# Where split weights begin inside their SBUF tiles: three lines or one, by unit and by part

## The chip, the core and the metric

The kernel runs on one core of a Trainium2 chip. The metric is the device time of one launch in microseconds (us); lower is better. Three runs of the kernel before gave 573.05, 573.16 and 573.88 us, median 573.16.

## What is computed

A decoder trunk of two layers on 256 tokens of width 1024, in float32. Layer 0 mixes tokens by a gated short convolution, layer 1 by causal attention with rotary positions (all 256 tokens lie in one block, so the block selection of the reference selects nothing more). Each layer ends in a gated MLP with a width-3 causal convolution. Cut to what matters:

```python
for i in range(DEPTH):                      # DEPTH = 2, D = 1024, D_FF = 2816
    h = rmsnorm(x, mix_norm[i])
    x = x + (short_conv_mixer(h, ...) if i == 0 else moba_attention(h, w_qkv, w_o))
    gu = causal_dwconv(rmsnorm(x, ffn_norm[i]) @ ffn_w_up[i], ffn_w_conv[i])
    g, u = split(gu, 2)
    x = x + (silu(g) * u) @ ffn_w_down[i]
return rmsnorm(x, final_norm)
```

## The kernel before

**Weights.** All weights lie in one array, cut into 201 units of 128 partitions by up to 1024 columns (`PLAN`), in the order in which they are used: the first and further units of the layer-0 mixer (`first`, `in`, `out`), the MLP of layer 0 (`up`, `down`), then `q`, `k` and `v` in four groups of four heads, then eight units `o`, then the MLP of layer 1. A chunk of two units is fetched by one DMA from the SP queue into a tile `raw`, four chunks ahead. `split_next` makes two float32r tiles of a unit: `hi` by a copy on ScalarE (ACT), `lo` = raw - hi by a subtraction on VectorE (DVE). Five tiles of each kind turn round (`SPLITS`).

**Products.** Every product is made of three matmuls, hi x hi, hi x lo and lo x hi (`passes`). The activations are split in the same way (`xh`/`xl`, `ps` and `o` with h and l). Where the weight is *held*, TensorE loads a 128 x 128 piece of the weight (LDWEIGHTS, the row PEld of the profile) and lets 256 columns of the activation run through it. In the stages `v` and `down` of layer 1 it is the other way: the weight is *streamed*, 512 columns at a time, and a 128 x 128 piece of the activation is loaded. These are `v_stage` and `TokenAccum.add`. A load runs beside the matmul before it.

**Places.** A tile of split weights is 1152 float32 columns long and begins at a multiple of 512 bytes. Inside it the 1024 columns of the weight begin some columns later: `HELD_AT` puts held weights at column 48 (hi) and 16 (lo), which is three and one lines of 64 bytes beyond the multiple of 512, and `STREAMED_AT` puts streamed ones at column 64, four lines, in both parts. A piece of 128 columns is 512 bytes long, so each piece of a unit stands at the same distance beyond a multiple of 512. All activations begin at such a multiple (`INPUTS_AT` is 0 throughout).

**Order.** Each engine executes its instructions in the order in which the code writes them (`InOrder` ties each instruction to the one before on its engine). In the attention, other kinds of matmul stand between the units of q, k, v and o: scores `s`, transposes `pt` and values `o` (not to be confused with the weights `o`, whose results are named `ao`). The MLP of layer 1 begins with ten units `up` (results `gu`) before its first unit `down` (results `fo`); from then on two units `up` and one unit `down` take turns.

The profile names nearly all instructions by one line, since a helper records them: tile names tell them apart. `qk`, `v`, `ao`, `gu`, `fo`, `cv`, `b` and `mo` are accumulators in PSUM.

Of the kernel before, what the change touches and what calls it, by code (L numbers as in the profile page):

```python
# [33 lines left out]
LINE = 128  # L34

HELD_AT = {"hi": 48, "lo": 16}
STREAMED_AT = {"hi": 64, "lo": 64}  # L40
INPUTS_AT = {0: 0, "out": 0, 1: 0, "down0": 0, 2: 0, "o": 0, 3: 0, "down1": 0}
NPS = 7
WARM = 8
# [9 lines left out]
def weight_plan():  # L53

    plan = [("first", n) for n in range(len(FIRST))]
    for j in range(ND):
        if j > 1:
            plan += [("in", 0, 1, j), ("in", 0, 2, j), ("in", 0, 0, j)]
        if j >= LAG_MIX:
            plan.append(("out", 0, j - LAG_MIX))  # L60
    plan += [("out", 0, j) for j in range(ND - LAG_MIX, ND)]
    for layer in range(2):
        if layer == 1:
            for g in range(GROUPS):
                plan += [(n, g, half) for n in "qk" for half in range(2)]
                if g in (0, GROUPS - 1):
                    plan += [("v", g // 2, c) for c in range(4)]
            plan += [("o", m) for m in range(ND)]
        for j in range(NF):
            plan += [("up", layer, 0, j), ("up", layer, 1, j)]  # L70
            if j >= LAG_FFN:
                plan.append(("down", layer, j - LAG_FFN))
        plan += [("down", layer, j) for j in range(NF - LAG_FFN, NF)]
    return plan


PLAN = weight_plan()
INDEX = {k: i for i, k in enumerate(PLAN)}
NU = len(PLAN)
WIDTH = [P * len(FIRST[k[1]][1]) if k[0] == "first" else U for k in PLAN]  # L80
CHUNKS = [[0, 1, 2, 3, 4], [5, 6], [7, 8], [9, 10]]
while CHUNKS[-1][-1] + 1 < NU:
    _s = CHUNKS[-1][-1] + 1
    CHUNKS.append(list(range(_s, min(_s + 2, NU))))
CHUNK_OF = {u: (c, sum(WIDTH[v] for v in us if v < u)) for c, us in enumerate(CHUNKS) for u in us}
CHUNK_WIDTH = [sum(WIDTH[u] for u in us) for us in CHUNKS]
CHUNK_START = [P * sum(CHUNK_WIDTH[:c]) for c in range(len(CHUNKS))]
# [29 lines left out]
def trunk(ctx: ExitStack, tc: tile.TileContext, x, wall, small, ropes, masks, final, out):  # L117
# [21 lines left out]
    def line(pool, w, off=0, dtype=F32, **kw):  # L139

        return pool.tile([P, -(-(off + w) // LINE) * LINE], dtype, **kw)[:, off : off + w]
# [14 lines left out]
    raw, hi, lo = {}, {}, {}  # L156

    def load_chunk():
        c = state["dma"]
        state["dma"] += 1  # L160
        w = CHUNK_WIDTH[c]
        raw[c] = wp.tile([P, w], F32, name=f"raw{c}", tag="raw", bufs=LOADS)
        s = CHUNK_START[c]
        src = wall[s : s + P * w].rearrange("(p f) -> p f", p=P)
        cuts = [CHUNK_OF[u][1] for u in CHUNKS[c]] + [w] if c < 4 else [0, w]
        for a, b in zip(cuts, cuts[1:]):
            Q.dma_start(raw[c][:, a:b], src[:, a:b])
# [10 lines left out]
    def split_next():  # L178
        u = state["split"]
        if u >= NU:  # L180
            return
        state["split"] += 1
        c, o = CHUNK_OF[u]
        while state["dma"] <= min(c + LOADS - 1, len(CHUNKS) - 1):
            load_chunk()
        w = WIDTH[u]
        src = raw[c][:, o : o + w]
        at = STREAMED_AT if PLAN[u][0] == "v" or PLAN[u][:2] == ("down", 1) else HELD_AT
        hi[u], lo[u] = (
            line(wp, U + 127 - at[n], at[n], F32R, name=f"{n}{u}", tag=n, bufs=SPLITS)[:, :w]  # L190
            for n in ("hi", "lo")
        )
        if u < 2:
            V.tensor_copy(hi[u], src)
            if u == 0:
                scaled(0, (0,), nm0)
                split_next()
                for v, part in ((0, src), (1, raw[0][:, P : 3 * P])):
                    V.tensor_sub(lo[v], part, hi[v].bitcast(F32))
            return  # L200
        S.activation(hi[u], src, AF.Copy)
        V.tensor_sub(lo[u], src, hi[u].bitcast(F32))

    def unit(key):
        u = INDEX[key]
        while state["split"] <= u:
            split_next()
        return hi[u], lo[u]
# [7 lines left out]
    def slot(splits=1):  # L216
        for _ in range(splits):
            split_next()
        for g in sorted(tasks, key=lambda g: g.__name__ == "rotate"):
            if next(g, StopIteration) is StopIteration:  # L220
                tasks.remove(g)
# [36 lines left out]
    def scaled(i, ms, nm):  # L258

        for m in ms:  # L260
            xh, xl = (
                line(ap_, T, INPUTS_AT[i], F32R, name=f"x{c}{i}_{m}", tag=f"x{c}{m}", bufs=1)
                for c in "hl"
            )
            S.activation(xh, xslice(m), AF.Copy, scale=gain(i, m))
            V.scalar_tensor_tensor(
                xl, xslice(m), gain(i, m), xh.bitcast(F32), op0=ALU.mult, op1=ALU.subtract
            )
            nm.xh[m], nm.xl[m] = xh, xl

    def prep(i, pair, nm, splits=2):
        scaled(i, (2 * pair, 2 * pair + 1), nm)
        if pair:
            square(i, pair - 1, nm)
        if pair == 3:
            square(i, pair, nm)
            sums = sum_squares(i, nm)
            next(sums)
            for _ in range(splits):
                split_next()  # L280
            next(sums, None)
# [628 lines left out]
```

## Time and profile before

| what | value |
|---|---|
| median of three runs | 573.16 us |
| the profiled execution, device time | 573.11 us |
| its span, first to last instruction | 571.3 us |
| TensorE (PE) busy | 564.7 us, 99% of the span |
| weight loads (PEld) busy | 544.5 us, 95% |
| VectorE busy | 469.5 us, 82% |
| ScalarE busy | 337.4 us, 59% |
| mean share of the DMA engines | 52.4% for the queue of the weights |
| granted clock of TensorE over the span | 0.999 |

Matmuls overlap one another: the duration of one is longer than the distance to the next. So a busy share of 99% does not tell how fast the matmuls follow each other; that is read from the starts of two matmuls in the timeline, divided by the number of matmuls from the one to the other.

### The profile page before, as it was taken

To read this page: it belongs to the slowest core of one execution; us is meant where nothing else is said; L and a number is where in the kernel's file an instruction comes from. 1 tells how busy PE (TensorE), PEld (TensorE's weight loads), DVE (VectorE), ACT (ScalarE), POOL (GpSimd) and SP (SyncE) were. 2 spreads that over 40 slices of the span, in tenths; PEclk is the share of its full clock that TensorE was granted. 3 is DMA by queue.
4 is the path that set the end of the run, shared out by engine and by line. 5 is a ranking of instruction groups with operands and counts; after the bars stand their busy time and mean duration, and the time that the engine had idled before them with its cause. 6 is when DMAs were issued, how large, how long until landed. Compare 5 with 4: busy or idle time off the path is not lost.

```text
span 571.3 us, 11291 instructions
## 1 busy us (share of the span) xinstructions
PE 564.7 (99%) x4628; PEld 544.5 (95%) x4628; DVE 469.5 (82%) x783; ACT 337.4 (59%) x556; POOL 8.8 (2%) x12
## 2 busy tenths in 40 slices
PE   9999999999999999999999999999999999999996
PEld 9999999999999999999989997999999999999994
DVE  5998767999988888886998887577999778878883
ACT  6655447567755555555937666565665555555553
POOL 0022010000000000000000000000000000000000
PEclk9999999999999999999999999999999999999999
DMA  8966552746755556556364334463466465555301
GB/s 296 384 216 238 205 205 89 263 154 231 263 177 211 204 170 217 178 192 220 91 247 169 97 139 148 148 231 112 177 220 231 176 220 163 206 204 172 142 1 73
DMA packets 17188, 106.86 MB, mean 187 GB/s; under 512 B 1904, under 2 KB 3056, under 8 KB 4976
## 3 DMA queue, kind: packets, MB, share of 16 engines
q1 hardware_dynamic: 16704, 105.60, 52.4%
q8 instruction: 36, 0.59, 0.4%
q10 hardware_dynamic: 432, 0.54, 0.3%
q14 instruction: 16, 0.13, 0.1%
HBM read 105.09 MB, written 1.05 MB: 186 GB/s over the span
## 4 chain that ended last, share of the span: by engine, by line
PE 99%; ACT 0%; DVE 0%; issue 0%
PE gu L100 42%; PE fo L100 21%; PE qk L100 8%; PE cv L100 8%; PE ao L100 4%; PE b L100 4%; PE v L100 4%; PE mo L100 4%; PE pt L100 1%; PE s L100 1%; PE o L100 1%; PE busy L100 1%; PE ss L100 0%; ACT of L100 0%; DVE of L100 0%; ACT sq L100 0%
## 5 line engine op out<-in xcount | busy, mean ns | idle before, releaser
L100 ACT ACTIVATE hi<-raw 128x1024 fp32r<-128x1024 f32 (+2 forms) x199 | 205.1, 1041 | 146.2 <-PE gu L100 78.9
L100 DVE TENSOR_TENSOR lo<-raw,hi 128x1024 fp32r<-128x1024 f32 (+3 forms) x201 | 239.7, 1200 | 54.9 <-ACT hi L100 54.7
L100 PE MATMUL gu<-xl,hi 128*128 128x256 f32 x704 | 194.9, 277 | 0.0
L100 PE MATMUL gu<-xh,hi 128*128 128x256 f32 x704 | 194.6, 276 | 0.0
L100 PE MATMUL gu<-xh,lo 128*128 128x256 f32 x704 | 194.6, 276 | 0.0
L100 PEld LDWEIGHTS gu<-xh,hi 128*128 128x128 f32 x704 | 132.2, 188 | 0.7
L100 PEld LDWEIGHTS gu<-xl,hi 128*128 128x128 f32 x704 | 132.1, 188 | 0.6
L100 PEld LDWEIGHTS gu<-xh,lo 128*128 128x128 f32 x704 | 132.1, 188 | 0.0
L100 DVE SCALAR_TENSOR_TENSOR gy<-gn,sm,gy 128x255 f32<-128x255 f32 (+1 forms) x176 | 80.8, 481 | 3.1
L100 ACT ACTIVATE gy<-gn,sm 128x256 f32<-128x256 f32 x88 | 39.3, 497 | 6.6 <-DVE gn L100 6.5
L100 PE MATMUL qk<-xh,hi 128*128 128x256 f32 x128 | 36.0, 281 | 0.0
L100 PE MATMUL qk<-xl,hi 128*128 128x256 f32 x128 | 35.6, 278 | 0.0
L100 PE MATMUL qk<-xh,lo 128*128 128x256 f32 x128 | 35.4, 277 | 0.0
L100 DVE TENSOR_TENSOR gn<-gu,rstd 128x512 f32<-128x512 f32 x44 | 30.1, 688 | 5.1 <-PE gu L100 5.1
L100 PE MATMUL cv<-xh,hi 128*128 128x256 f32 x128 | 33.4, 282 | 0.0
L100 PE MATMUL cv<-xl,hi 128*128 128x256 f32 x128 | 32.9, 278 | 0.0
L100 PE MATMUL cv<-xh,lo 128*128 128x256 f32 x128 | 32.9, 278 | 0.0
L100 PEld LDWEIGHTS qk<-xh,hi 128*128 128x128 f32 x128 | 24.0, 188 | 0.5 <-issue 0.3
L100 PEld LDWEIGHTS qk<-xl,hi 128*128 128x128 f32 x128 | 24.0, 188 | 0.0
L100 PEld LDWEIGHTS qk<-xh,lo 128*128 128x128 f32 x128 | 24.0, 188 | 0.0
L100 ACT ACTIVATE s<-gy 128x256 f32<-128x256 f32 x44 | 17.9, 406 | 9.8 <-DVE gy L100 9.7
L100 PEld LDWEIGHTS cv<-xh,hi 128*128 128x128 f32 x128 | 23.4, 192 | 0.1
(474 smaller groups left out, 1075.1 us busy)
## 6 DMA issues: line engine op xcount, KB each, us to landing
raw<-wall SPq DMA_DIRECT2D x95, 1024.0 KB, 4.7
raw<-wall SPq DMA_DIRECT2D x6, 384.0 KB, 6.5
xt<-x SPq DMA_DIRECT2D x3, 256.0 KB, 6.0
out<-of SPq DMA_DIRECT2D x3, 256.0 KB, 2.1
raw<-wall SPq DMA_DIRECT2D x3, 192.0 KB, 4.1
gain_row<-final SPq DMA_DIRECT2D x1, 512.0 KB, 5.7
rope<-ropes SPq DMA_DIRECT2D x1, 384.0 KB, 5.3
out<-of ACTq DMA_DIRECT2D x1, 256.0 KB, 2.4
```

What stands on the lines that cost most here:

```text
L100: r = f(*args, **kw)
```

## The change

A function `weights_at` takes the place of the two tables. It gives the column at which a part of a unit begins: 16 (one line) where `second` is true, else 48 (three lines). For units q, k and o, `second` is whether the last number of the unit's name is odd (for q and k the half of the head columns, for o the output block): both parts of a unit begin at the same column, 48 in one unit and 16 in the next. For all other units hi begins at 48 and lo at 16. So the held units `first`, `in`, `out`, `up` and layer 0's `down` keep their places; q, k and o (24 units) get equal parts; the streamed units, 8 of `v` and 22 of layer 1's `down`, go from 64/64 to 48/16.

```diff
-HELD_AT = {"hi": 48, "lo": 16}
-STREAMED_AT = {"hi": 64, "lo": 64}
...
+def weights_at(u, part):
+    n = PLAN[u]
+    second = n[-1] % 2 if n[0] in "qko" else part == "lo"
+    return 16 if second else 48
...
-        at = STREAMED_AT if PLAN[u][0] == "v" or PLAN[u][:2] == ("down", 1) else HELD_AT
+        at = {n: weights_at(u, n) for n in ("hi", "lo")}
         hi[u], lo[u] = (
             line(wp, U + 127 - at[n], at[n], F32R, name=f"{n}{u}", tag=n, bufs=SPLITS)[:, :w]
```

The tile stays 1152 columns long whatever the column is (1024 + 127 rounded up to a multiple of 128), so no other tile moves. The built programs have the same instructions in the same order on every engine, with the same shapes; only start addresses of split weights differ.

## Rows read from the trace of the kernel before

**Rows 1.** The page's parts 1 and 4: span, busy time (share) xinstructions, chain's shares.
```profile
span 571.3 us, 11291 instructions
...
PE 564.7 (99%) x4628; PEld 544.5 (95%) x4628; DVE 469.5 (82%) x783; ACT 337.4 (59%) x556; POOL 8.8 (2%) x12
...
PE 99%; ACT 0%; DVE 0%; issue 0%
```

**Rows 2.** Waits of PE, whole span: waiter <- waited for: us in total, times, longest.
```profile
PE busy L100 <- DVE eps L100: 1.1, 1, 1.1
```

**Rows 3.** Waits of all engines, whole span.
```profile
ACT hi L100 <- PE gu L100: 78.9, 58, 1.5
...
ACT hi L100 <- DMA raw<-wall: 4.2, 3, 1.9
```

**Rows 4.** Timeline of PE, MLP of layer 0: start us, duration us, operation, count.
```profile
139.75 0.28 PE L100 MATMUL gu<-xh,hi 128*128 128x256 f32 x1
...
255.01 0.28 PE L100 MATMUL gu<-xh,hi 128*128 128x256 f32 x1
```

**Rows 5.** Timeline of PE from the o units to the end of layer 1's first `up` units.
```profile
361.11 0.28 PE L100 MATMUL ao<-oh,hi 128*128 128x256 f32 x1
...
410.80 0.28 PE L100 MATMUL gu<-xh,lo 128*128 128x256 f32 x1
```

**Rows 6.** Groups of PE, 133 to 267 us, then 382 to 408: xcount | busy, mean ns.
```profile
L100 PE MATMUL gu<-xl,hi 128*128 128x256 f32 x253 | 69.8, 276 | 0.0
...
L100 PE MATMUL gu<-xl,hi 128*128 128x256 f32 x72 | 20.4, 283 | 0.0
```

**Rows 7.** Timeline of PE, q and k units of groups 2 and 3.
```profile
309.81 0.28 PE L100 MATMUL qk<-xh,hi 128*128 128x256 f32 x1
...
312.18 0.28 PE L100 MATMUL qk<-xh,lo 128*128 128x256 f32 x1
...
331.74 0.28 PE L100 MATMUL qk<-xh,hi 128*128 128x256 f32 x1
...
339.83 0.28 PE L100 MATMUL qk<-xh,lo 128*128 128x256 f32 x1
```

**Rows 8.** Timeline of PE, layer 0's `first` stage, six columns of one unit.
```profile
10.40 0.40 PE L100 MATMUL cv<-xh,hi 128*128 128x256 f32 x2
...
11.46 0.39 PE L100 MATMUL cv<-xh,lo 128*128 128x256 f32 x2
...
12.14 0.39 PE L100 MATMUL cv<-xh,hi 128*128 128x256 f32 x2
```

**Rows 9.** Timeline of PE, one streamed unit `down` between units `up`.
```profile
453.63 0.40 PE L100 MATMUL fo<-hi,ps_5h 128*128 128x512 f32 x1
453.86 0.40 PE L100 MATMUL fo<-hi,ps_5l 128*128 128x512 f32 x1
454.10 0.39 PE L100 MATMUL fo<-lo,ps_5h 128*128 128x512 f32 x1
...
455.01 0.39 PE L100 MATMUL fo<-hi,ps_5h 128*128 128x512 f32 x1
...
456.37 0.28 PE L100 MATMUL gu<-xh,hi 128*128 128x256 f32 x1
...
456.72 0.28 PE L100 MATMUL gu<-xh,hi 128*128 128x256 f32 x1
```

**Rows 10.** Groups of ACT and DVE, 133 to 267 us, then 412 to 560.
```profile
L100 ACT ACTIVATE hi<-raw 128x1024 fp32r<-128x1024 f32 x51 | 54.0, 1060 | 48.8 <-PE gu L100 35.6 <-PE fo L100 13.1
L100 DVE TENSOR_TENSOR lo<-raw,hi 128x1024 fp32r<-128x1024 f32 x52 | 63.5, 1222 | 16.5 <-ACT hi L100 16.5
...
L100 ACT ACTIVATE hi<-raw 128x1024 fp32r<-128x1024 f32 x53 | 56.1, 1059 | 52.8 <-PE gu L100 42.0 <-PE fo L100 10.8
L100 DVE TENSOR_TENSOR lo<-raw,hi 128x1024 fp32r<-128x1024 f32 x54 | 66.0, 1222 | 17.8 <-ACT hi L100 17.8
```

**Rows 11.** Timeline, the last matmul.
```profile
565.35 0.39 PE L100 MATMUL fo<-lo,ps_21h 128*128 128x512 f32 x1
```

## The prediction

> **What bounds the kernel now.** I read the page first: of a span of 571.3 us TensorE is busy for 564.7, and the chain that ended last is TensorE's for 99% [rows 1]. The waits come next: TensorE waits for another engine once, 1.1 us, before its first warm-up matmul [rows 2]. The longest wait of the others is ScalarE's for TensorE, 78.9 us before it may overwrite a `hi` tile, while it waits for landing weights 4.2 us in all [rows 3]. So the others have room, and the time is the sum of the distances between matmuls. The change can reach it only through these distances; the reader's task is to find where they are not the same.
>
> They are read from starts. In layer 0's MLP the matmul at 139.75 and the one at 255.01 stand 1017 matmuls of 256 columns apart: 115.26 us / 1017 = 113.33 ns each [rows 4]. I call this the tight pace. From the second half of the first o unit to the end of layer 1's first ten `up` units the starts 361.11 and 410.80 are 418 matmuls of the same shape apart: 49.69 / 418 = 118.88 ns, the loose pace, 5.55 ns more each [rows 5]. The forms are the same, the `up` units even have the same columns 48 and 16, and nothing is waited for. The duration shows it too: 276 ns for `gu<-xl,hi` in layer 0, 283 here [rows 6]. Both run at the granted clock of 0.999, the upper of its two levels.
>
> In q and k the pace changes by stretches: 331.74 to 339.83 holds 68 distances, 119.0 ns each, and 309.81 to 312.18 holds 20, 118.5 ns each [rows 7]. The rest of q and k is tight, with a lost matmul or so at each change to scores, transposes or values. So the loose pace is a state: a stretch begins after another kind of matmul, and then it keeps itself up. The longest one is carried out of the o units through ten `up` units and ends where the first `down` unit begins. Streamed units show a third thing: after `up`, the first six matmuls take 455.01 - 453.63 = 1.38 us, 230 ns each, and the next six 1.36 us, 226.7 each, which is twice 113.33; the three `up` matmuls after them take 0.35 us instead of 0.34 [rows 9].
>
> **The change, part by part.** *Instructions.* None is added, removed or moved on any engine, and no DMA; shapes stay. Writing the split parts costs the same at either place: hi 1060 ns and lo 1222 ns in layer 0 (columns 48/16), 1059 and 1222 in layer 1, where a third of the units begin at 64 [rows 10]. I take 0 for it. What covers a nanosecond more on these engines is their waiting, 48.8 us of ScalarE's before `hi` in 134 us [rows 10]; if it were gone, TensorE would wait for weights.
>
> *Equal parts in q, k and o.* Why should this matter to a state that keeps itself up? The trace of before has one place where the weights' column stays the same over many matmuls: layer 0's `first` units, where all six columns of hi run before lo. After a pause it falls into the loose pace: from 10.40 to 11.46 nine matmuls on hi (column 48) take 1.06 us, 117.8 ns each. At the first lo (column 16) the pace is tight: 11.46 to 12.14 holds six in 0.68 us, 113.3 each, and it stays tight when hi comes back [rows 8]. So a run at column 48 holds the loose pace and a run at column 16 ended it at once, whereas in hi, hi, lo by turns a single matmul at 16 does not end it [rows 5]. One case is thin evidence, and I count it so in the chances. With the change every second unit of q, k and o is a run of up to 24 matmuls at column 16. By this reading a loose stretch lives to the next odd unit at most:
>
> - o and the ten `up` units: 418 matmuls x 5.55 ns = 2.32 us now [rows 5]. The even unit o0 keeps some 6 loose matmuls before o1 begins (0.03 us); then it is tight, and layer 1's `up` units, whose columns don't change, start tight and stay so as in layer 0. Gain 2.29 us.
> - q and k from 331.74: 68 x 5.6 = 0.38 us [rows 7]. The first of the three units is odd; I leave 6 matmuls, 0.03. Gain 0.35 us.
> - q of group 2 from 309.81: an even unit, which holds the pace. Gain 0 (the bound is 20 x 5.2 = 0.10).
>
> What is late next where this gain goes? Nothing that these rows show: ScalarE and VectorE wait for TensorE in these stages too. The tail behind the last matmul at 565.35 stays as it is [rows 11].
>
> *Streamed weights at 48/16 instead of 64/64.* There are 352 streamed matmuls (88 x 3 in `down`, 32 x 3 in `v`). No row shows weights streaming from columns 48 and 16. From below: at best the dear beginnings vanish, 18 units behind `up` units with 6 x 3.3 + 10 = 30 ns each, 0.54 us [rows 9]. From above: the dearest distance there, 454.10 - 453.86 = 0.24 us against 0.227, 13 ns more, in all 352: 4.6 us [rows 9]. Held weights at 48/16 against activations at 0 run tight over 1017 matmuls [rows 4], and streamed ones at 64 do after six; both pairs are the nearest rows to the new one, so I take 0, with the dear beginnings as they are.
>
> *A rule against it.* The trace has TensorE at two paces on the same shapes. The Trainium skill, page "SBUF — State Buffer", section "Who interferes with whom", gives TensorE two independent read ports, one for the streaming operand and one for weight loads, and says that it never waits on anyone. By that page the place of a weight costs nothing, and the time would stay at 573.1. The trace disagrees with it so far as some 500 matmuls run 5.55 ns slower without a named wait; that the place is the reason is not shown by it.
>
> *Sum.* Profiled execution 573.11 us (span 571.3 and 1.8 around it) - 2.29 - 0.35 = 570.47 us. The profiled execution itself lies 0.05 us below the median of the runs, which needs no correction. Forecast 570.5.
>
> **The rivals.** *A: the pace does not hang on where q, k and o lie.* The loose pace comes from the pauses at scores, transposes and values, which the change leaves, and goes as it came. For it: layer 1's `up` units are loose at the same columns at which layer 0's are tight, and stretches begin and end at the same kinds of pause. Against it: the place of rows 8, where the pace changed inside a unit, without a pause, at the step from 48 to 16. Time: as before, 573.1, with 0.6 either way for stretches that fall otherwise, as the three runs differ by 0.8.
>
> *B: the forecast holds in q, k and o, but streamed weights pay.* If the mean of the dear beginnings, 3.3 ns, became the rule in 352 matmuls, 1.2 us; at the loose pace's 11 ns for 512 columns, 3.9 us. Time: 570.5 + 1.2 to 3.9 = 571.7 to 574.4; it cancels the forecast from (2.64 - 1.15) / 352 = 4.2 ns on. For it: lo and hi streamed from different columns change the distance between the two reads at each third matmul. Against it: held weights do the same in layer 0 at no cost.
>
> *C: equal parts lock the loose pace in.* The alternation of hi and lo is then what lets the tight pace last, and q, k and o run loose in all 576 matmuls (24 units x 24) instead of some 280 now; o hands it on to the `up` units as today. Price: 296 x 5.55 ns = 1.6 us; time 574.8. It is slower than the bound from 1.15 / 0.00555 = 207 more loose matmuls on. For it: in rows 8 the nine matmuls on hi alone stayed loose throughout. Against it: the six on lo alone did not, and tight stayed tight on hi alone afterwards.
>
> *D: half of it.* The o units shed the loose pace, but a pause behind them, or the two norm matmuls in the `up` units, brings it back; a gain of 1.2 to 2 us, 571.1 to 571.9.
>
> **How the numbers follow.** The forecast has 0.47 (569.5 to 571.1), D 0.10, A 0.18, B 0.12, C 0.13. A measurement of this kernel can tell some 0.2%, 1.15 us, from no change: below 572.0 is faster, above 574.3 slower. Faster: 0.47 + 0.10 + a third of B = 0.61. Slower: C, and a little of A and B, 0.15. Within: 0.24. The range takes in the forecast with its lower end (all loose stretches and the dear beginnings gone: 573.11 - 2.32 - 0.38 - 0.10 - 0.54 = 569.8, and 0.4 below it for the spread of runs), D, A and most of B, and leaves out C: 569.4 to 574.0.
>
> **What would show it.** Right: the starts of the `gu` matmuls in layer 1 before the first `fo` stand 113.3 ns apart, mean duration 276 and not 283; the same in `ao` from the second o unit on and in `qk` of group 3; in odd units no distance of 118 after the first few. The streamed part is right if the first six `fo` matmuls behind `up` take 1.36 to 1.38 us and the next six 1.36. Wrong: a loose stretch that runs through an odd unit (A or C), 118 ns in a unit of q or k that was tight (C), `fo` distances above 227 ns to the end of a unit (B). Any wait of TensorE for another engine beyond the first would make the whole reading wrong.

## Result and profile after

The changed kernel takes 576.46 us (median of four runs, 576.15 to 576.77) against 573.16 for the kernel before: a ratio of 1.0057, 95% interval 1.0043 to 1.0071, so 3.3 us slower. The forecast was 570.5, with a range of 569.4 to 574.0. Some executions of several kernels, the one before among them, are 11 to 12 us longer than the rest; medians and ratios leave them out, and of the traces only that of e10 is of such an execution.

The profiled execution takes 576.60 us, 3.49 more than that of before. The page's parts 1 and 4 (columns as in [rows 1]):

```profile
span 574.8 us, 11291 instructions
...
PE 567.8 (99%) x4628; PEld 546.3 (95%) x4628; DVE 469.8 (82%) x783; ACT 337.9 (59%) x556; POOL 8.8 (2%) x12
...
PE 99%; DVE 0%; ACT 0%; issue 0%
```

The waits of TensorE, to be held against [rows 2]:

```profile
PE busy L110 <- DVE eps L110: 1.1, 1, 1.1
PE mo L110 <- DVE ys0l L110: 0.3, 1, 0.3
```

The counts of instructions are the same, the chain is TensorE's as before, and the one new wait is 0.3 us in layer 0. The time is again in the distances between matmuls.

**What came as forecast.** Timeline of PE (start, duration), from the o units to the last of the first ten `up` units, the stretch of [rows 5]:

```profile
361.68 0.28 PE L110 MATMUL ao<-oh,hi 128*128 128x256 f32 x1
...
409.06 0.28 PE L110 MATMUL gu<-xh,lo 128*128 128x256 f32 x1
```

47.38 us for the same 418 distances: 113.3 ns each, where [rows 5] had 118.88. The loose stretch is gone, and with it 2.3 us.

**What came against it.** The same timeline at the same `down` unit as [rows 9], with the two `up` units ahead of it:

```profile
447.65 0.28 PE L110 MATMUL gu<-xh,hi 128*128 128x256 f32 x1
...
453.36 0.39 PE L110 MATMUL fo<-hi,ps_5h 128*128 128x512 f32 x1
...
454.75 0.39 PE L110 MATMUL fo<-hi,ps_5h 128*128 128x512 f32 x1
...
456.14 0.28 PE L110 MATMUL gu<-xh,hi 128*128 128x256 f32 x1
```

The first six `fo` take 1.39 us and the next six 1.39 too, some 232 ns each; in [rows 9] the second six had come down to 226.7. The 48 matmuls of the `up` units take 5.71 us, 119.0 ns each: the loose pace, where before they were tight but for their first few. Groups of PE from 412 to 560 us (xcount | busy, mean ns), the form of [rows 6]:

```profile
L110 PE MATMUL gu<-xl,hi 128*128 128x256 f32 x272 | 77.0, 283 | 0.0
L110 PE MATMUL gu<-xh,hi 128*128 128x256 f32 x272 | 75.8, 279 | 0.0
L110 PE MATMUL gu<-xh,lo 128*128 128x256 f32 x272 | 75.8, 279 | 0.0
```

283 is the mark of the loose pace that [rows 6] showed for `gu<-xl,hi` ahead of the first `down`. Here the same form has it behind the first `down`, and by their starts all 34 `up` units there (816 matmuls in the three forms) are loose. The last matmul starts at 568.84 us, 3.49 later than in [rows 11]:

```profile
568.84 0.40 PE L110 MATMUL fo<-lo,ps_21h 128*128 128x512 f32 x1
```

Summing by stage what each distance has over 113.33 ns (256 columns) or 226.67 ns (512), for distances 2 to 20 ns too long, gives the account of one profiled execution of each kernel, in us. The last three columns are experiments from below.

| stage, layer 1 | before | after | e1 | e2 | e3 |
|---|---|---|---|---|---|
| q, k | 0.55 | 0.51 | 0.30 | 1.08 | 0.41 |
| v | 0.10 | 0.45 | 0.12 | 0.43 | 0.62 |
| o | 1.02 | 0.04 | 0.04 | 1.06 | 0.07 |
| first ten `up` | 1.33 | 0 | 0 | 1.33 | 0 |
| `down` | 0.45 | 1.34 | 0.47 | 1.34 | 1.66 |
| 34 `up` between `down` | 0.10 | 4.50 | 0.11 | 4.50 | 2.36 |
| sum | 3.55 | 6.84 | 1.04 | 9.74 | 5.12 |

From before to after q, k, o and the ten `up` give 2.35 us; v and `down` take 1.24, and the `up` units between the `down` units 4.40. Net 3.29 of the measured 3.49; the new wait in layer 0 is of the size of the rest.

### The profile page after: what moved, and what is told of

Read it like the earlier page. It is cut to its first block, busy times and chain, and to the rows that moved or that the text cites. A ratio compares the mean times of both kernels' runs of the same rounds, so it can differ in the third digit from the quotient of the medians.

```text
span 574.8 us, 11291 instructions
## 1 busy us (share of the span) xinstructions
PE 567.8 (99%) x4628; PEld 546.3 (95%) x4628; DVE 469.8 (82%) x783; ACT 337.9 (59%) x556; POOL 8.8 (2%) x12
## 4 chain that ended last, share of the span: by engine, by line
PE 99%; DVE 0%; ACT 0%; issue 0%
PE gu L110 42%; PE fo L110 21%; PE qk L110 8%; PE cv L110 8%; PE v L110 4%; PE ao L110 4%; PE b L110 4%; PE mo L110 4%; PE pt L110 1%; PE s L110 1%; PE o L110 1%; PE busy L110 1%; PE ss L110 0%; ACT of L110 0%; DVE of L110 0%; ACT sq L110 0%
```

## Experiments

All edits stand in `weights_at` of the changed kernel, and one more in `INPUTS_AT`. The theory that I formed from the account: the part on q, k and o does what was forecast, and the streamed weights both run dearer and hand the loose pace to the `up` units behind them. Its rival: the equal parts of q, k and o put TensorE into another state from there on, and the streamed places are innocent.

**e1, q, k and o alone.** Streamed weights stay at 64.

```diff
+    if n[0] == "v" or n[:2] == ("down", 1):
+        return 64
```

> Only q, k and o change their places, as in the changed kernel; streamed weights stay at column 64 in both parts. Theory (the streamed part alone makes the changed kernel slower, the q/k/o part does what was forecast): o from its second unit on and the first ten up units of layer 1 at 113.3 ns, the down units of layer 1 as in the kernel before (230 ns for the first six matmuls, then 226.7), time 573.16 - 2.3 = 570.9 us, 570.3 to 571.5. Rival (the two parts act together: a tight start into the first down unit is what makes the down and up units loose, whatever the streamed columns are): up units loose behind each down unit, 34 x 133 ns = 4.5 us more than the theory, 575 us.

Measured: 570.76 us (570.63 to 571.02) against 573.24, ratio 0.9957 [0.9942, 0.9972]. Timeline of PE at the same `down` unit, then the groups of PE from 412 to 560 us:

```profile
451.53 0.40 PE L112 MATMUL fo<-hi,ps_5h 128*128 128x512 f32 x1
...
452.92 0.39 PE L112 MATMUL fo<-hi,ps_5h 128*128 128x512 f32 x1
...
454.28 0.28 PE L112 MATMUL gu<-xh,hi 128*128 128x256 f32 x1
```

```profile
L112 PE MATMUL gu<-xl,hi 128*128 128x256 f32 x272 | 75.1, 276 | 0.0
```

1.39 and then 1.36 us, as in [rows 9], and 276 ns behind: the streamed stage is that of before. The rival falls. This version is faster than both kernels.

**e2, streamed weights alone.** q, k and o as before, streamed ones at 48/16.

```diff
-    second = n[-1] % 2 if n[0] in "qko" else part == "lo"
-    return 16 if second else 48
+    return 16 if part == "lo" else 48
```

> Only the streamed weights change their places, to 48 and 16; q, k and o stay at 48 and 16. Theory: the changed kernel lies 3.4 us above the one before and the q/k/o part gains 2.3, so this one lies 3.4 + 2.3 = 5.7 us above: 578.9 us, 578 to 579.6; all up units of layer 1 loose, 5.5 ns each, streamed matmuls 231 to 232 ns in the mean to the end of their stages. Rival (both parts act together): the first ten up units are loose as before and nothing is handed over, so 573 to 574.5 us.

Measured: 578.16 us (577.03 to 579.01), ratio 1.0079 [1.0062, 1.0096]. Groups of PE from 382 to 408 us, and from 418 to 560:

```profile
L108 PE MATMUL gu<-xl,hi 128*128 128x256 f32 x70 | 19.8, 283 | 0.0
```

```profile
L108 PE MATMUL gu<-xl,hi 128*128 128x256 f32 x267 | 75.6, 283 | 0.0
```

Loose before the first `down` as in [rows 6], and loose behind it as in the kernel after. e1 and e2 add up only roughly: -2.5 and +4.9 us, by their own runs of before, make +2.4 against +3.3 for both. The four runs of e2 lie apart, two near 577.2 and two near 579.0, and its trace is of one at 578.97; by the account the halves give -2.51 and +6.19, together 3.68 against 3.29. In that trace q and k are looser than before, 1.08 us, without a change of theirs: their loose stretches are not fixed by their places alone.

**e3, e4, e5: what is wrong with 48/16.** Either that hi and lo stream from unequal columns, or the columns themselves. Each is e1 with another number for streamed weights: 48, 16 or 0 in both parts (e3 shown).

```diff
+    if n[0] == "v" or n[:2] == ("down", 1):
+        return 48
```

> q, k and o as in the changed kernel, streamed weights at column 48 in both parts, so that hi and lo stream from the same distance. Theory of the unequal parts (it is the change of distance between hi and lo, at each third matmul, that keeps the streamed matmuls loose): streamed matmuls settle at 226.7 ns as with 64 and 64, the up units stay tight, 570.9 us. Theory of the column (48 is a bad place for a streamed weight against an activation at 0): streamed matmuls above 229 ns to the end of a unit, up units loose behind them, 575 to 578 us.

Measured: 574.9 us (574.39 to 575.17), ratio 1.0028 [1.0018, 1.0038]. Groups of PE from 412 to 560 us:

```profile
L112 PE MATMUL gu<-xl,hi 128*128 128x256 f32 x272 | 76.1, 280 | 0.0
```

Equal parts don't help, so the columns matter. `down` costs 20 ns per three matmuls more, 1.66 us in all; the `up` units came out loose in every second pair, hence the mean of 280.

> As the kernel with only q, k and o changed (570.8 us), but streamed weights at column 16 in both parts, one line from the place of the loaded activations. Theory of the distance (four lines between the loaded and the streamed operand are harmless, one or three are not): streamed matmuls stay above 229 ns to the end of a unit, and up units behind them are loose at least in part: 573 to 577 us. Rival (only 48 is a bad column for streaming): 226.7 ns after the first six, 570.8 us.

Measured: 576.03 us (575.82 to 576.18), ratio 1.0051 [1.0022, 1.0081]. The same groups:

```profile
L112 PE MATMUL gu<-xl,hi 128*128 128x256 f32 x272 | 77.0, 283 | 0.0
```

Column 16 costs little in `down` itself, about 7 ns per three, 0.83 us in all against 0.45 before (the first half of `v` paid 20 ns per three at the same distance), yet all 34 `up` units behind are loose (4.45 us).

> The same with streamed weights at column 0 in both parts, the same place beyond a multiple of 512 bytes as the loaded activations. Theory of the distance: no distance at all is as bad as one or three lines or worse, 573 to 578 us, streamed matmuls above 229 ns throughout. Rival (only an offset of an odd number of lines is bad, an even one is free): 226.7 ns after the first six, 570.8 us.

Measured: 570.63 us (570.33 to 571.24), ratio 0.9957 [0.9941, 0.9973], and the groups:

```profile
L112 PE MATMUL gu<-xl,hi 128*128 128x256 f32 x272 | 75.1, 276 | 0.0
```

Column 0 is as good as 64. My guess that nearness to the activation's place costs fell with it: distances of 0 and 4 lines are free here, 1 and 3 are not.

**e10 and e9: distance or place.** The loaded operand in `down` is the activation, at column 0. In e10 it moves to 16, with streamed weights at 64, three lines apart; in e9 the weights of `down` move to 80 as well, four lines apart.

```diff
-INPUTS_AT = {..., "down1": 0}
+INPUTS_AT = {..., "down1": 16}
...
+    if n[0] == "v" or n[:2] == ("down", 1):
+        return 64                              # e10
+        return 64 if n[0] == "v" else 80       # e9
```

> The kernel with only q, k and o changed (570.8 us), streamed weights at column 64 as there, but the split activations that down of layer 1 loads begin at column 16, one line beyond a multiple of 512, so that the distance is three lines as with weights at 48 and activations at 0. v keeps its distance of four. Theory of the distance: down is loose to the end of each unit (1.1 us more than at distance four, as with 48 and 48) and hands the loose pace to up units (2 us more): 573 to 575 us, v tight. Rival (it is the absolute place of the streamed weight): all as at 64 and 0, 570.8 us.

Measured: 576.57 us, a single run; the trace is of another execution, of 587.74 us. Timeline of PE, one `down` unit:

```profile
438.62 0.39 PE L112 MATMUL fo<-hi,ps_2h 128*128 128x512 f32 x1
...
440.02 0.39 PE L112 MATMUL fo<-hi,ps_2h 128*128 128x512 f32 x1
...
441.42 0.28 PE L112 MATMUL gu<-xh,hi 128*128 128x256 f32 x1
```

Six in 1.40 us and the next six in 1.40: `down` pays 20 ns per three, as in e3, with which it shares the distance of three lines and neither column. The place alone is not the reason. The time was above what I expected of the distance, since all `up` units behind came out loose (4.56 us). By the code, the tiles `ps` of these activations grow from 256 to 384 columns with the new start, in e10 and e9 alike, so that other tiles may stand elsewhere by multiples of 512 bytes; no run separates this.

> The same with the activations that down of layer 1 loads at column 16 and its streamed weights at column 80: both operands moved by one line, the distance is four lines again. Theory of the distance: down and up as in the kernel with only q, k and o changed, 226.7 ns after the first six, 570.8 us. Rival (absolute places of the weights): five lines from a multiple of 512 is an odd place like 16 and 48, loose, 573 to 577 us.

Measured: 575.14 us (575.06 to 575.73), ratio 1.0037 [1.0017, 1.0056]. Timeline of PE, one `down` unit; groups from 412 to 560 us:

```profile
427.89 0.39 PE L112 MATMUL fo<-hi,ps_2h 128*128 128x512 f32 x1
...
428.59 0.39 PE L112 MATMUL fo<-hi,ps_2h 128*128 128x512 f32 x1
...
429.95 0.39 PE L112 MATMUL fo<-hi,ps_2h 128*128 128x512 f32 x1
...
430.63 0.28 PE L112 MATMUL gu<-xh,hi 128*128 128x256 f32 x1
```

```profile
L112 PE MATMUL gu<-xl,hi 128*128 128x256 f32 x272 | 76.9, 283 | 0.0
```

Half a hit. With four lines between them again, `down` settles: after three matmuls in 0.70 us six take 1.36, 226.7 each, and its sum is 0.41 us as before. So with e10 and e3 it is the distance between the two operands that goes with the pace of `down`, and not the column of either. But the `up` units behind are loose, 4.49 us. A dear `down` is thus not needed for the hand-over. I missed the time by 4, and it lies in the range of the rival, whose reason the pace of `down` refutes.

**e6, another way to stop the hand-over.** The kernel after, with layer 1's `up` units also in equal parts, 48 and 16 in turn.

```diff
-    second = n[-1] % 2 if n[0] in "qko" else part == "lo"
+    second = n[-1] % 2 if n[0] in "qko" else n[2] if n[:2] == ("up", 1) else part == "lo"
```

> The changed kernel, and layer 1's up units with equal parts too: the gate half at 48 in both, the other half at 16 in both. Streamed weights stay at 48 and 16. Theory (a loose stretch that a down unit hands over ends at the step from a unit at 48 to a unit at 16): of each pair of up units behind a down unit the first is loose, 24 x 4.4 = 106 ns, the second tight, so 17 pairs gain 17 x (266 - 106) = 2.7 us: 576.6 - 2.7 = 573.9 us. Rival (equal parts change nothing in a loose stretch): both units loose at 4.4 ns, 17 x (266 - 212) = 0.9 us: 575.7 us.

Measured: 573.55 us, ratio 1.0006 [0.9997, 1.0016]. Timeline of PE, the two `up` units between two `down` units:

```profile
421.79 0.28 PE L110 MATMUL gu<-xh,hi 128*128 128x256 f32 x1
...
424.62 0.28 PE L110 MATMUL gu<-xh,hi 128*128 128x256 f32 x1
...
427.34 0.39 PE L110 MATMUL fo<-hi,ps_2h 128*128 128x512 f32 x1
```

The first 24 matmuls, on column 48, take 2.83 us, 117.9 ns each; the next 24, on column 16, 2.72 us, 113.3 each. All 17 pairs do so, give or take three matmuls: each `down` hands over the loose pace, and each step from 48 to 16 ends it. Of the 4.50 us of the `up` units 1.81 are left.

**e7, e8, e12: is it the step or the column?** e7 is e1 with q, k and o all at 48, e8 with all at 16; neither has a step in these units (the lines of the edit that keep streamed weights at 64, as in e1, are left out).

```diff
-    second = n[-1] % 2 if n[0] in "qko" else part == "lo"
+    second = n[0] not in "qko" and part == "lo"     # e7
+    second = n[0] in "qko" or part == "lo"          # e8
```

> Streamed weights at column 64 as before; q, k and o at column 48 in both parts in every unit, so equal parts, but no step from a unit at 48 to a unit at 16. Theory of the step (only the step from 48 to 16 ends a loose stretch without a pause): what is loose after the last pause before the o units stays loose at 4.4 ns through them and goes on at 5.5 in the first ten up units; 572.3 to 573.2 us. Rival (equal parts end it): o from the second unit on and the ten up units tight, 570.8 us.

Measured: 571.18 us, a single run, against 573.27. Timeline of PE, the q and k units of [rows 7]'s second stretch, then the o units from behind the pause in o0:

```profile
332.14 0.28 PE L112 MATMUL qk<-xh,hi 128*128 128x256 f32 x1
...
340.14 0.28 PE L112 MATMUL qk<-xh,lo 128*128 128x256 f32 x1
```

```profile
361.49 0.28 PE L112 MATMUL ao<-oh,hi 128*128 128x256 f32 x1
...
381.55 0.28 PE L112 MATMUL gu<-xh,hi 128*128 128x256 f32 x1
```

68 distances in 8.00 us, 117.6 each: with no step, the stretch stays loose through all three units, as expected. The time is below what I expected since the o units came tight out of the pause in o0, without a step: 177 distances in 20.06 us, 113.3 each, and the ten `up` units behind are tight too. That is the larger part of e1's gain, with no unit at 16.

> The same with q, k and o at column 16 in both parts in every unit. Theory of the step: no step from 48 to 16 here either, a loose stretch that begins in the o units lasts through the first ten up units, 572.3 to 573.2 us. Rival (a run at column 16 ends it): tight after a few matmuls of each unit, 570.3 to 570.8 us.

Measured: 573.06 us (572.58 to 573.33), ratio 0.9996 [0.9986, 1.0007]. Timeline of PE, o units:

```profile
361.50 0.28 PE L112 MATMUL ao<-oh,hi 128*128 128x256 f32 x1
...
382.35 0.28 PE L112 MATMUL gu<-xh,hi 128*128 128x256 f32 x1
```

177 distances in 20.85 us, 117.8 each, all on column 16, and the ten `up` units behind are loose too (1.33 us). Column 16 alone does not end it here; the gain of the change is gone. The kernel after says the same in the q and k units of [rows 7]'s second stretch, an odd, an even and an odd unit (timeline of PE):

```profile
332.31 0.28 PE L110 MATMUL qk<-xh,hi 128*128 128x256 f32 x1
...
334.78 0.28 PE L110 MATMUL qk<-xh,hi 128*128 128x256 f32 x1
...
337.61 0.28 PE L110 MATMUL qk<-xh,hi 128*128 128x256 f32 x1
...
339.99 0.28 PE L110 MATMUL qk<-xh,hi 128*128 128x256 f32 x1
```

The odd unit, on 16, is loose (21 distances, 2.47 us, 117.6 each), so is the even one on 48 (24 in 2.83), and the odd one behind it is tight (21 in 2.38, 113.3). The step from 48 to 16 ends it, the step from 16 to 48 does not.

In the kernels so far the pace of the o units goes with the column of o0, though no run changes o0 alone. In all nine with both parts of o0 at 48 (after, e1, e3 to e7, e9, e10) the o units are tight within six matmuls of the pause; with 48 and 16 by turns (before, e2) or both at 16 (e8) they stay loose.

e12 gives every held unit equal parts, 48 and 16 in turn, with streamed weights at 64: if the step always helps, layer 0 and the rest should be tight.

```diff
+    if n[0] == "v" or n[:2] == ("down", 1):
+        return 64
-    second = n[-1] % 2 if n[0] in "qko" else part == "lo"
-    return 16 if second else 48
+    return 16 if u % 2 else 48
```

> Streamed weights at column 64; every held unit, of layer 0 too, has equal parts, 48 where its number in the plan is even and 16 where it is odd. Theory of the step: a loose stretch ends at the next step from 48 to 16 wherever it begins, so the time is that of the kernel with only q, k and o changed, 570.8 us, give or take 0.5 for q and k; and no run is longer by some 11 us, since the stretch that made one run of another kernel 586 us long (loose from layer 0's mixer through its whole MLP) cannot last. Rival (the alternation of hi and lo is what keeps layer 0 tight): loose units in layer 0, up to 576 x 3 matmuls x 4.4 ns = 7.6 us more, 573 to 578 us.

Measured: 573.85 us (573.24 to 574.34), ratio 1.0009 [1.0000, 1.0019]. Timeline of PE, a pair of `up` units up to the next `down`:

```profile
421.67 0.28 PE L111 MATMUL gu<-xh,hi 128*128 128x256 f32 x1
...
427.32 0.40 PE L111 MATMUL fo<-hi,ps_2h 128*128 128x512 f32 x1
```

Layer 0 was tight, but this pair, the first unit at 16 and the second at 48, takes 5.65 us for 48 matmuls, 117.7 each, though `down` streams from 64 as in e1. The `up` units between `down` units cost 2.79 us in all, 0.11 in e1. Behind `down`, a unit with equal parts stays loose until the next step from 48 to 16, where hi and lo by turns at 48 and 16 recovers within a few matmuls. In the nine pairs of 48 and then 16 the second unit turns tight after three matmuls, in the eight of 16 and then 48 neither does. So the step did what I expected of it; what I missed is that half of the pairs have none. The rival, a loose layer 0, did not happen, though the time lies in its range.

**e11, four lines for held weights too.** If only odd distances were bad, all weights at column 64 should do.

```diff
-    n = PLAN[u]
-    second = n[-1] % 2 if n[0] in "qko" else part == "lo"
-    return 16 if second else 48
+    return 64
```

> All weights, held and streamed, at column 64 in both parts, four lines from the activations at 0; no operand at an odd number of lines. Theory (the loose pace needs an operand at an odd number of lines): no distance above 114 ns outside the changes to other kinds of matmul, in q, k, o and up too; 570.2 to 570.8 us. Rival (held weights are another case: at an even number of lines they are loose always, some 4,000 matmuls x 5.5 ns = 22 us): 585 to 596 us.

Measured: 595.82 us (595.74 to 595.9), ratio 1.0392 [1.0371, 1.0413]. Groups of PE from 133 to 267 us, and a timeline there:

```profile
L108 PE MATMUL gu<-xl,hi 128*128 128x256 f32 x249 | 70.5, 283 | 0.0
L108 PE MATMUL gu<-xh,lo 128*128 128x256 f32 x249 | 70.5, 283 | 0.0
```

```profile
138.81 0.28 PE L108 MATMUL gu<-xh,hi 128*128 128x256 f32 x1
...
139.89 0.28 PE L108 MATMUL gu<-xh,hi 128*128 128x256 f32 x1
```

Nine matmuls in 1.08 us, 120.0 each; the account has this pace in every held stage of both layers, while `down` and `v` stay at 0.45 and 0.12 us. The theory fell and its rival held: the column that is free for a streamed weight is the worst of those tried for a held one.

## Why the prediction was wrong

- **What bounds the kernel** was right: the one new wait, which the prediction had named as a sign against it, is 0.3 us of 3.49, and the account above finds the rest in distances between matmuls.
- **Equal parts in q, k and o** was right in size and wrong in its reason, so the size was luck in part: forecast -2.64, measured -2.5 in e1. The 2.29 us of o and the ten `up` units came whole, but not as forecast, by o1 at column 16 ending what o0 keeps up: in the kernel after and in e1 o0 is tight straight from its pause, at column 48, and e7 has the same without any unit at 16. The text had it that a run at column 16 ends the loose pace; e8 shows 177 matmuls on 16 that stay loose. Where a stretch did end, it was at the step from 48 to 16, in [rows 8] as in e6. In q and k 0.25 us came in e1 and 0.04 in the kernel after, of 0.35: in the latter the first, odd unit of [rows 7]'s second stretch stayed loose and only the third turned tight.
- **Streamed weights at 48/16, taken as 0,** is the step that failed. "Both pairs are the nearest rows to the new one" took two rows as neighbours that are not: the tight 1017 matmuls of [rows 4] hold the weight and stream the activation, and in `down` the roles are reversed; e11 shows how little one says of the other. The streamed ones at 64 stood four lines from the activation, and e3 and e4 show three lines and one to be dearer than four. Measured, v and `down` pay 1.24 us, 3.5 ns in each of 352, within the bounds given.
- **The term that was not there** is the larger one: 4.40 us in 816 `up` matmuls behind the `down` units, which the change does not touch. The upper bound of 4.6 us counted streamed matmuls alone. The prediction had the parts for it: a loose pace that keeps itself up, carried from o into `up` units of the same columns [rows 5], and three slower `up` matmuls behind each `down` [rows 9]. It asked only where the loose pace ends, at the first `down`, and not what a `down` of another place would start.
- **Rival B** named the right stage, though not for the reason it gave, that lo and hi stream from different columns: e3 has equal columns and is no cheaper. Its low end, 1.2 us, is about the price of the streamed weights themselves, and its time of up to 574.4 lacked the hand-over. Of the signs named ahead, `fo` distances above 227 ns to the end of a unit are what the trace shows. **C**, the rival on the slower side, didn't happen in sum, q and k being 0.51 us loose where they were 0.55. But its sign, 118 ns in a unit that was tight, came once, in the first q unit of group 1: 23 distances took 2.61 us before, 113.5 each, and take 2.71 after, 117.8 each, all on column 48 in the kernel after (lines below). **D** falls with e1, and so does **A** for o and the `up` units; in q and k e2 bears it out, where stretches fell otherwise at the same places.
- **The rule on two ports.** Weight places alone moved this kernel between 570.8 us (e1) and 595.8 (e11), with no wait of TensorE in the records beyond the first, of 1.1 us, and one of 1.0 us in e11. The Trainium skill, page "SBUF — State Buffer", section "Who interferes with whom", gives TensorE independent read ports and lets it wait on nobody. As the prediction took it, that the place of a weight costs nothing, these runs disagree with it, whatever the mechanism inside is.

The unit in which C's sign came, timeline of PE, before and then after:

```profile
297.36 0.28 PE L100 MATMUL qk<-xl,hi 128*128 128x256 f32 x1
...
299.97 0.28 PE L100 MATMUL qk<-xh,hi 128*128 128x256 f32 x1
```

```profile
297.85 0.28 PE L110 MATMUL qk<-xl,hi 128*128 128x256 f32 x1
...
300.56 0.28 PE L110 MATMUL qk<-xh,hi 128*128 128x256 f32 x1
```

**Still open:** why the step from 48 to 16 ends a loose pace between units, while hi and lo by turns step so at each third matmul and stay loose [rows 5]; why o0 leaves its pause tight at 48 and not at 16; why the `up` units of e9 are loose behind a `down` that is not; and whether two reads of TensorE meet or its reads meet the writes of ScalarE and VectorE. No run separates the last two.

## What to carry to other kernels

Where one engine bounds the time with no waits, take the distances between its instructions stage by stage, and look for the same shape at two paces. Before reusing a place that is good for one operand, ask whether it is loaded or streamed there, and count the stage behind as well: here the untouched `up` units cost more than three times what the moved weights did. Change one family of tiles at a time, since e1 alone was worth 2.5 us that the other half of the change buried. And where a gain comes out as forecast, take the supposed cause away as e7 does, before the reason is believed.

## What the runs showed of the chip

- Matmuls of one shape, at a granted clock of 0.997 to 1.000 over the span, have two paces, 113.3 and 117.6 to 120.0 ns for 256 columns. With held weights three and one lines beyond the activation's place, either pace lasts over hundreds of matmuls; with four lines (e11) only 120.0 occurs.
- For streamed weights the distance to the loaded operand counts: 0 and 4 lines run at 226.7 ns (e1, e5, e9), 3 lines at 20 ns more per three (e3, e10), 1 line at 7 to 20 more (e4).
- Between held units of layer 1 that follow each other without a pause, the loose pace ended, within three matmuls, at all 34 steps from column 48 to 16 that the traces hold. Of 11 steps from 16 to 48 it went on at 10; at one (o1 of e12) it ended in the middle of the second unit. In layer 0's `first` units, behind the pause of [rows 8], the first step to 16 ended it in nine traces and only the second in those of e6 and e10.
